# A Trainium2 encoder trunk: head order of the key-query products, and the depth of a low-rank matmul

## Chip, cores and metric

The kernel runs on one core of a Trainium2 chip. The metric is the time of one execution on the device, in microseconds, lower being better. Times of several executions are given by their median. The profile shows one further execution, recorded by the hardware profiler.

## What is computed

Two layers over 2048 tokens of width 1024. Layer A mixes the tokens with a recurrence (RWKV-7), twelve heads of width 64, beside a cross-attention into 256 memory tokens; layer B uses differential attention instead. This case concerns layer A alone:

```python
def rwkv7_time_mix(z, mu, w0, w2, a0, a2, k_k, k_a, r_k, lnx_w, lnx_b):
    ...
    z = z + (token_shift(z) - z) * mu
    r, k, v, wd, ad = jnp.split(z, [BR_W, 2 * BR_W, 3 * BR_W, 3 * BR_W + LORA_W], axis=-1)
    w = -jax.nn.softplus(-(w0 + jnp.tanh(wd) @ w2)) - 0.5
    decay = jnp.exp(-jnp.exp(w))
    a = jax.nn.sigmoid(a0 + ad @ a2)
    ...
    def step(state, inp):
        r_t, w_t, k_t, v_t, kk_t, a_t = inp
        sa = jnp.einsum('bhvk,bhk->bhv', state, -kk_t)
        state = (state * w_t[:, :, None, :]
                 + sa[..., None] * (kk_t * a_t)[:, :, None, :]
                 + v_t[..., None] * k_t[:, :, None, :])
        y_t = jnp.einsum('bhvk,bhk->bhv', state, r_t)
        return state, y_t
```

`tanh(wd) @ w2` and `ad @ a2` are the two low-rank products of depth 64. The kernel computes the recurrence in chunks of 64 tokens: inside a chunk it needs the products of keys with queries, 128x128 for each head.

## The kernel before

Layer A is made of 24 steps. A step takes one pair of heads (two heads are the 128 partitions) and one block of 512 tokens, which is eight chunks. The steps run over two halves of the sequence, in each over six head pairs, and for each pair over two blocks, called b=0 and b=1 here. Weights are loaded for a pair in its b=0 step.

A step has these parts. `p1` (from L312) makes its inputs: projections through `pj` (L174, 24 matmuls of 128x512 each, in three passes of rounded parts: high by high, low by high, high by low), the two low-rank products `lr` (L323, L324), and from them the decays, summed by a scan (L330). `p2` (from L371) makes the key-query products `pg` (L380): for each half g of the eight chunks and each head hh one PSUM bank of four products, which DVE then reads (L383), scaled and masked, into `Gm`; two banks come in turn. It also transposes keys and values. `p3` inverts the small triangular matrices of the chunks: on DVE from L431 to L461, with products on PE of 64x64 (`inv`, L455) and 32x32 (`invz`, L468, which needs the transposed block `Ta` of L461, and `invr`, L474). `p4` (from L482) is the recurrence, eight chunks in a row: `xy` (L493, L496), copied by ACT (L498), `us` (L502), copied by DVE (L503), `sps` (L507), added to the state by DVE (L510), and `xy` of the next chunk. `p5` normalises and writes out.

The code calls, for each i, `p4` and `p5` of step i, `p2` and `p3` of step i+1, and `filler(i+2)`, which does `p1` of step i+2 and a gate projection. A scheduler of the language then sets the order on each engine; each engine works through its own list in order. So on PE the chunks of `p4` have products of other parts between them, which cover the waits for ACT and DVE. PSUM has eight banks: two for `pg` and the other small results, two for `xy`, one for `us` and `sps`, three for `pj` and `lr`.

The low-rank operands: `th[i]` (128x512) holds the high part of one input and its low part, in 64 rows each (`lora_in`). `load_lora` (L568) makes a tile `lora` of three 128x128 slots: slots 0 and 1 are the high parts of `w2` and `a2`, each twice, one above the other; slot 2 holds the low part of `w2` in rows 0 to 63 and that of `a2` in rows 64 to 127. So L323 multiplies the weights' high part by the input's high and low, over 128 rows, and L324 adds the weights' low part by the input's high, over 64 rows.

Of the kernel before, what the change touches and what calls it, by code (L numbers as in the profile page):

```python
# [15 lines left out]
P = 128  # L16
# [9 lines left out]
TB = 512  # L26
# [33 lines left out]
def hybrid_kernel(ctx, tc, S, HALF, x, mem, pv, cv, dist, postn, w_out, w_mkv, a_w, w2, a2, w_kv, b_w, out):  # L60
# [47 lines left out]
    def split_w(pool, src, gain, hi, lo, eng=G_, raws=None, tag="wraw", bufs=RAWS):  # L108
        """weights from DRAM as hi + lo"""
# [19 lines left out]
    def rstd_(xt, junk, ss):  # L129
        """junk: where the squares go; ss: a column for each part of the rows"""  # L130
        for i, (x_, j_) in enumerate(zip(xt, junk)):
            A.activation(j_, x_, AF.Square, accum_out=ss[:, i:i + 1])
        if len(xt) > 1:
            V.tensor_tensor(out=ss[:, 0:1], in0=ss[:, 0:1], in1=ss[:, 1:2], op=ALU.add)

    def rows_T(xt, ps, dst, eng):
        """512 columns of 128 rows, transposed, to each hi, lo of dst, with its gain; eng rounds to hi"""
# [13 lines left out]
    def norm_T(rows, dst, pool, W, PS, xt=None, ptag="gm", eng=nc.sync, junk=None):  # L151
        """128 rows of DRAM (or xt), normalised and transposed into each hi, lo of dst, with its gain"""
# [26 lines left out]
    def mem_T(h, m0, W, PS, pool):  # L179
        """the memory, normalised for both layers, transposed"""  # L180
# [4 lines left out]
    def mem_kv(h, tile_, W, load, PS):  # L185
        """for both layers, keys (hi over lo) and values of the memory, to DRAM"""
# [22 lines left out]
    def layer_a(ph):  # L209
# [96 lines left out]
        class Step:  # L306
            """one head pair, one block of TB tokens"""
# [4 lines left out]
            def p1(self):  # L312
# [7 lines left out]
                for i, e in enumerate((cum[:, :, 1:65], asg.rearrange("p (c t) -> p c t", t=C))):  # L320
                    pl = PS([P, TB], "lr", "pj")
                    rows = slice(i * 64, i * 64 + 64)
                    mm(pl, lhsT=lora[:, i], rhs=th[i], start=True, stop=False)  # L323
                    mm(pl, lhsT=lora[rows, 2], rhs=th[i][rows], start=False, stop=True)  # L324
# [24 lines left out]
                # AR: even chunk (r|a), odd (a|r);  BK: even (k|b), odd (b|k)  # L349
# [7 lines left out]
                # 1 + (a - 1) k_a  # L357
# [13 lines left out]
            def p2(self):  # L371
                p, rn, AR, BK = self.p, self.rn, self.AR, self.BK
                Gm = T([P, 2, NJ, 2, P], "Gm", 2)
                for g in range(2):
                    for hh in range(2):
                        pg = PS([P, 4, P], "pg")
                        hs = slice(hh * 64, hh * 64 + 64)
                        for c4 in range(4):
                            c = g * 4 + c4
                            mm(pg[:, c4, :], lhsT=BK[hs, c, :], rhs=AR[hs, c, :], start=True, stop=True)  # L380
                        for c4 in range(4):
                            c = g * 4 + c4
                            V.scalar_tensor_tensor(out=Gm[:, c % 2, c // 2, hh, :], in0=pg[:, c4, :], scalar=rn[:, c, hh:hh + 1],  # L383
                                                   in1=cc("maskE" if c % 2 == 0 else "maskO", 128), op0=ALU.mult, op1=ALU.mult)
                # BK transposed, rows scaled
# [23 lines left out]
            def p3(self):  # L409
                Gm = self.Gm  # L410
                # N = strict upper part: odd rows 0:64 cols 0:64, even rows 64:128 cols 64:128
# [22 lines left out]
                # X1[p, t, (ib, i)] = T[t, i];  X2[p, i, (tb, t)] = T[t, i]  # L434
# [11 lines left out]
                # TT32 = TT16 + TT16 E1 TT16, E1 between the 16 x 16 blocks of each 32 x 32 one  # L446
# [12 lines left out]
                # the 32 x 32 blocks a (first) and b of each chunk: TT[a, b] = TT[a, a] N[a, b] TT[b, b]  # L459
# [22 lines left out]
            def p4(self):  # L482
# [3 lines left out]
                for c in range(NC):  # L486
                    j, e = c // 2, c % 2
                    ar = slice(64, 128) if e == 0 else slice(0, 64)   # alpha / U rows
                    rr = slice(0, 64) if e == 0 else slice(64, 128)   # r / V rows
# [62 lines left out]
        def lora_in(w18, half, b):  # L552
# [7 lines left out]
            # hi over lo for the one, lo over hi for the other  # L560
# [7 lines left out]
        def load_lora(p):  # L568
            """hi of both, twice; lo of the one over lo of the other"""
# [4 lines left out]
            l = pw.tile([P, 3, P], F32R, name="lora", tag="lora", bufs=1)  # L574
            A.activation(l[:, 0:2], raw, AF.Copy)
            for i in range(2):
                rows = slice(i * 64, i * 64 + 64)
                G_.tensor_tensor(out=l[rows, 2], in0=raw[rows, i], in1=l[rows, i].bitcast(F32), op=ALU.subtract)
# [5 lines left out]
        def filler(idx):  # L584
            """what the lookahead of step idx traces: its inputs and projections"""
# [96 lines left out]
    def store_q(l, m, b, ps, gate, W):  # L682
        """queries (hi, lo) and gates of two heads of the memory attention, TB tokens, to DRAM"""
# [593 lines left out]
```

## Time and profile before

| | |
|---|---|
| three runs | 3231.21, 3232.57 and 3237.78 us; median 3232.57 us |
| profiled execution, span | 3242.7 us, its own time; 10.1 us above the median |
| PE busy | 3074.5 us, 95% of the span |
| DVE, ACT, POOL busy | 2008.1, 1421.3, 928.4 us |
| chain that ended last | PE 76%, DVE 14%, ACT 4% |
| mean granted TensorE clock | 0.977 of full |

PE (TensorE) is the engine of the matmuls, DVE VectorE, ACT ScalarE, POOL GpSimd. The busy times overlap; the chain that ended last is followed back from the last instruction, at each step to what released it. L380 means line 380 of the kernel. Layer A takes about the first 1560 us of the span.

### The profile page before, as it was taken

The page shows a single profiled execution, that of the slowest core. Times are in us where ns is not written, and L with a number is a line of the kernel's source. Part 1 is how long each engine was busy: PE and PEld are TensorE (multiplying, and loading weights), DVE is VectorE, ACT ScalarE, POOL GpSimd, SP SyncE. Part 2 cuts the span into 40 slices and gives each one's busy share as a digit, 9 for nine tenths or more (in the row PEclk, how much of TensorE's full clock was granted, in tenths as well). Part 3 has the DMA queues.
Part 4 walks back from the last instruction along what each step waited for, and adds up shares of the span by engine and source line. Part 5 has one row for each costly group of instructions (what it writes and reads, how often), then busy time and mean ns, then how long its engine had stood idle before and what let it go on. Part 6 is the DMA issues. An engine that isn't in the chain of part 4 may idle for free.

```text
span 3242.7 us, 53751 instructions
## 1 busy us (share of the span) xinstructions
PE 3074.5 (95%) x20026; PEld 2404.1 (74%) x20026; DVE 2008.1 (62%) x5546; ACT 1421.3 (44%) x3126; POOL 928.4 (29%) x1092
## 2 busy tenths in 40 slices
PE   6899999998899999999899999999999999999999
PEld 4766767676667676767577798898887878877777
DVE  6678777866687878786456411111106888887554
ACT  6524333434443434333345522222315777777443
POOL 3224434443244334433100121312411332222100
PEclk9989999998899999999899999999999999999999
DMA  4201000113210001002554443423436555444453
GB/s 131 75 16 35 27 22 22 34 40 90 57 35 27 23 22 33 29 18 69 136 147 135 134 113 90 117 74 96 117 110 159 118 116 112 102 85 119 118 154 113
DMA packets 266150, 265.21 MB, mean 82 GB/s; under 512 B 16832, under 2 KB 206656, under 8 KB 265760
## 3 DMA queue, kind: packets, MB, share of 16 engines
q1 hardware_dynamic: 237760, 195.31, 20.7%
q0 software_dynamic: 28128, 66.46, 10.1%
q8 instruction: 157, 2.57, 0.3%
q14 instruction: 105, 0.86, 0.1%
HBM read 180.45 MB, written 81.26 MB: 81 GB/s over the span
## 4 chain that ended last, share of the span: by engine, by line
PE 76%; DVE 14%; ACT 4%; issue 3%; DMA 2%; POOL 1%; SPq 0%; DVEq 0%; ACTq 0%; POOLq 0%
PE pj L174 30%; PE po L820 10%; PE o L1135 5%; PE vps L996 4%; PE pg L380 3%; PE s L1094 3%; PE s L1095 2%; PE us L502 2%; PE xy L496 2%; PE tr L1125 2%; PE sps L507 1%; PE xy L493 1%; PE mo L759 1%; PE xy L513 1%; DVE E L1097 1%
## 5 line engine op out<-in xcount | busy, mean ns | idle before, releaser
L174 PE MATMUL pj<-hhi,wh 128*128 128x512 f32 x928 | 395.3, 426 | 2.2 <-DVE hlo L149 1.7
L174 PE MATMUL pj<-hhi,wl 128*128 128x512 f32 x928 | 393.2, 424 | 0.4 <-POOL wl L123 0.4
L174 PE MATMUL pj<-hlo,wh 128*128 128x512 f32 x928 | 385.0, 415 | 0.0
L123 POOL TENSOR_TENSOR wl<-wraw,wh 128x512 fp32r<-128x512 f32 x168 | 221.0, 1327 | 399.8 <-ACT wh L122 372.2
L1097 DVE CUSTOM_DVE_ANT_0 E<-s,dist 128x512 f32<-128x512 f32 (+1 forms) x480 | 276.2, 605 | 35.0 <-PE s L1095 28.9
L174 PE MATMUL pj<-bh,wh 128*128 128x512 f32 x672 | 262.6, 391 | 0.0
L174 PE MATMUL pj<-bl,wh 128*128 128x512 f32 x672 | 262.4, 391 | 0.0
L174 PE MATMUL pj<-bh,wl 128*128 128x512 f32 x672 | 262.3, 390 | 0.0
L1102 ACT ACTIVATE E<-E,nm 128x1920 f32<-128x1920 f32 (+7 forms) x192 | 229.4, 1199 | 59.1 <-DVE nm L1100 58.6
L491 POOL TENSOR_SCALAR SP<-sb,PC 128x128 f32<-128x128 f32 x192 | 119.5, 624 | 469.7 <-DVE sb L510 469.7
L1135 PE MATMUL o<-th,vs 128*128 128x256 f32 (+1 forms) x864 | 211.0, 376 | 2.3 <-ACT th L1128 0.9
L174 PEld LDWEIGHTS pj<-hhi,wh 128*128 128x128 f32 x928 | 178.5, 192 | 45.6 <-ACT hhi L148 3.3
L1094 PE MATMUL s<-ks,qd 128*128 128x512 f32 (+1 forms) x480 | 205.7, 432 | 2.2 <-DVE mx L1097 1.2
L174 PEld LDWEIGHTS pj<-hhi,wl 128*128 128x128 f32 x928 | 177.6, 191 | 38.9 <-POOL wl L123 0.8
L174 PEld LDWEIGHTS pj<-hlo,wh 128*128 128x128 f32 x928 | 178.2, 192 | 33.9 <-issue 0.2
L122 ACT ACTIVATE wh<-wraw 128x512 fp32r<-128x512 f32 x168 | 105.4, 628 | 198.0 <-PE pj L174 138.9
L1135 PEld LDWEIGHTS o<-th,vs 128*128 128x128 f32 x864 | 153.8, 189 | 38.7 <-ACT th L1128 19.4
L514 ACT ACTIVATE ys<-xy 64x128 f32<-64x128 f32 x192 | 52.0, 271 | 297.0 <-PE xy L513 251.5
L1095 PE MATMUL s<-ks,qd 128*128 128x512 f32 (+1 forms) x480 | 176.2, 373 | 0.0
L510 DVE SCALAR_TENSOR_TENSOR sb<-sps,PC,SP 64x64 f32<-64x64 f32 x384 | 108.4, 282 | 64.9 <-PE sps L507 57.0
L174 PEld LDWEIGHTS pj<-bh,wh 128*128 128x128 f32 x672 | 126.6, 188 | 26.4 <-DVE ot L831 0.3
L174 PEld LDWEIGHTS pj<-bl,wh 128*128 128x128 f32 x672 | 126.6, 188 | 26.2
(401 smaller groups left out, 7342.3 us busy)
## 6 DMA issues: line engine op xcount, KB each, us to landing
wraw<-in_a_w SPq DMA_DIRECT2D x126, 256.0 KB, 2.9
qd<-qd_d POOLq DMA_DIRECT2D x48, 512.0 KB, 6.9
mq<-mq POOLq DMA_DIRECT2D x64, 256.0 KB, 4.3
ks<-ks_d POOLq DMA_DIRECT2D x24, 512.0 KB, 6.5
yr<-y_dram SPq DMA_DIRECT2D x31, 384.0 KB, 4.9
xt<-in_x SPq DMA_DIRECT2D x16, 512.0 KB, 5.3
x_dram<-ot SPq DMA_DIRECT2D x16, 512.0 KB, 4.4
wraw<-in_b_w SPq DMA_DIRECT2D x32, 256.0 KB, 3.0
```

Of the source, the lines that this page charges most:

```text
L122: A.activation(hi[:, ks], raw, AF.Copy)
L123: eng.tensor_tensor(out=lo[:, ks], in0=raw, in1=hi[:, ks].bitcast(F32), op=ALU.subtract)
L174: mm(ps, lhsT=w[a_][:, k, wcol], rhs=h[b_][:, k, tsl], start=n == 0, stop=n == 3 * KT - 1)
L491: G_.tensor_scalar(out=SP, in0=SB, scalar1=PC[:, c:c + 1], scalar2=None, op0=ALU.mult)
L510: V.scalar_tensor_tensor(out=SB[hc, hc], in0=sp[hc, :], scalar=PC[hc, c:c + 1], in1=SP[hc, hc], op0=ALU.mult, op1=ALU.add)
L820: mm(po[hf], lhsT=a_[:, k, :], rhs=b_[hf][:, k, :], start=k == i == 0, stop=k == KT - 1 and i == 2)
L996: mm(ps[:, t, :], lhsT=hT[b][a_][:, k, tsl], rhs=w[b_][:, k, :], start=n == 0, stop=n == 3 * KT - 1)
L1094: mm(ps[:, f:f + w_], lhsT=qd[:, 0, c, qs], rhs=k_[:, c, 0:w_], start=True, stop=False)
L1095: mm(ps[:, f:f + w_], lhsT=qd[:, 1, c, qs], rhs=k_[:, c, 0:w_], start=False, stop=True)
L1097: V.tensor_tensor_reduce(out=e[:, kb * 512:kb * 512 + w], in0=ps[:, 0:w], in1=dt_[:, u0:u0 + w], scale=-SLOPES[h], scalar=3.0e38, op0=ALU. ...
L1102: A.activation(E[c][:, 0:nk], E[c][:, 0:nk], AF.Exp, bias=nm[:, c:c + 1], scale=-1.0, accum_out=nm[:, 2 + c:3 + c])
L1135: mm(po[:, oc], lhsT=vs[kt // 4][:, kt % 4, :], rhs=th[:, rc], start=n == 0, stop=n >= nmm - 2, skip_group_check=True)
```

## The change

There are three parts. In `p2` both banks of a half are allocated together and the matmuls take the two heads in turn; DVE's readings keep their order, head 0's four and then head 1's four. In `p1` and `load_lora` the second low-rank matmul uses 128 rows: the tile has four slots, slots 2 and 3 hold the low parts of `w2` and `a2`, each twice, and the product gains the term low by low. One POOL subtraction over 128x256 takes the place of two over 64x128. And `ones` and `epsd`, two small constants of layer B, come from a pool that is opened behind layer A; the two DVE operations that fill them then run there. The line numbers of the changed kernel are smaller by one in `p1` from L323 on (L323, L324 and L330 are now L322, L323 and L329); L380 is now L379, and L383 to L513 differ by at most one. Comments that went are left out here.

```diff
                 for i, e in enumerate((cum[:, :, 1:65], asg.rearrange("p (c t) -> p c t", t=C))):
                     pl = PS([P, TB], "lr", "pj")
-                    rows = slice(i * 64, i * 64 + 64)
                     mm(pl, lhsT=lora[:, i], rhs=th[i], start=True, stop=False)
-                    mm(pl, lhsT=lora[rows, 2], rhs=th[i][rows], start=False, stop=True)
+                    mm(pl, lhsT=lora[:, 2 + i], rhs=th[i], start=False, stop=True)
...
                 for g in range(2):
+                    pgs = [PS([P, 4, P], "pg") for hh in range(2)]
+                    for c4 in range(4):
+                        for hh in range(2):
+                            hs = slice(hh * 64, hh * 64 + 64)
+                            mm(pgs[hh][:, c4, :], lhsT=BK[hs, g * 4 + c4, :], rhs=AR[hs, g * 4 + c4, :], start=True, stop=True)
                     for hh in range(2):
-                        pg = PS([P, 4, P], "pg")
-                        hs = slice(hh * 64, hh * 64 + 64)
                         for c4 in range(4):
                             c = g * 4 + c4
-                            mm(pg[:, c4, :], lhsT=BK[hs, c, :], rhs=AR[hs, c, :], start=True, stop=True)
-                        for c4 in range(4):
-                            c = g * 4 + c4
-                            V.scalar_tensor_tensor(out=Gm[:, c % 2, c // 2, hh, :], in0=pg[:, c4, :], scalar=rn[:, c, hh:hh + 1],
+                            V.scalar_tensor_tensor(out=Gm[:, c % 2, c // 2, hh, :], in0=pgs[hh][:, c4, :], scalar=rn[:, c, hh:hh + 1],
                                                    in1=cc("maskE" if c % 2 == 0 else "maskO", 128), op0=ALU.mult, op1=ALU.mult)
...
-            l = pw.tile([P, 3, P], F32R, name="lora", tag="lora", bufs=1)
+            l = pw.tile([P, 4, P], F32R, name="lora", tag="lora", bufs=1)
             A.activation(l[:, 0:2], raw, AF.Copy)
-            for i in range(2):
-                rows = slice(i * 64, i * 64 + 64)
-                G_.tensor_tensor(out=l[rows, 2], in0=raw[rows, i], in1=l[rows, i].bitcast(F32), op=ALU.subtract)
+            G_.tensor_tensor(out=l[:, 2:4], in0=raw, in1=l[:, 0:2].bitcast(F32), op=ALU.subtract)
...
-    ones = const.tile([P, P], F32, name="ones")
-    epsd = const.tile([P, P], F32, name="epsd")
...
     op = layer_a(ph.enter_context(pool_(name="ph", bufs=NB)))
+    const2 = ctx.enter_context(pool_(name="const2", bufs=1, side="right"))
+    ones = const2.tile([P, P], F32, name="ones")
+    epsd = const2.tile([P, P], F32, name="epsd")
```

What the scheduler makes of it is seen in the order of instructions on an engine. First PE, at the start of a stretch of the recurrence beside which a b=0 step is prepared. The names are those of the code, with numbers of the buffers: two numbers of `pg` are the two heads' banks. Before:

```order
L380 MATMUL pg_5911<-AR_5648,BK_5649 128x128 x3
L502 MATMUL us_5729<-xs_5727,TT_5419 64x64 x2
L380 MATMUL pg_5911<-AR_5648,BK_5649 128x128
L380 MATMUL pg_5920<-AR_5648,BK_5649 128x128 x4
L507 MATMUL sps_5733<-UV_5338,BKT_5325 64x64 x2
...
L380 MATMUL pg_5929<-AR_5648,BK_5649 128x128
L502 MATMUL us_5749<-xs_5747,TT_5419 64x64 x2
L380 MATMUL pg_5929<-AR_5648,BK_5649 128x128 x3
L507 MATMUL sps_5753<-UV_5338,BKT_5325 64x64 x2
L513 MATMUL xy_5743<-UV_5338,Gm_5288 64x64 x2
L380 MATMUL pg_5938<-AR_5648,BK_5649 128x128 x4
```

And now:

```order
L379 MATMUL pg_5904<-AR_5641,BK_5642 128x128
L379 MATMUL pg_5905<-AR_5641,BK_5642 128x128
L379 MATMUL pg_5904<-AR_5641,BK_5642 128x128
L502 MATMUL us_5722<-xs_5720,TT_5413 64x64 x2
L379 MATMUL pg_5905<-AR_5641,BK_5642 128x128
L379 MATMUL pg_5904<-AR_5641,BK_5642 128x128
L379 MATMUL pg_5905<-AR_5641,BK_5642 128x128
L379 MATMUL pg_5904<-AR_5641,BK_5642 128x128
L379 MATMUL pg_5905<-AR_5641,BK_5642 128x128
...
L379 MATMUL pg_5922<-AR_5641,BK_5642 128x128 x3
...
L379 MATMUL pg_5923<-AR_5641,BK_5642 128x128 x3
...
L379 MATMUL pg_5923<-AR_5641,BK_5642 128x128
```

In the first half (5911 and 5920 before, 5904 and 5905 now) the heads alternate; in the second half (5929 and 5938 before, 5922 and 5923 now) head 0's four still come ahead of head 1's four, and head 1's four are now parted by the next chunk.

Second, PE at the end of such a stretch, behind the last `sps` of a step. Before:

```order
L507 MATMUL sps<-UV,BKT 64x64 x2
...
L323 MATMUL lr<-th_1322,lora 128x512
L324 MATMUL lr<-th_1322,lora 128x512
L323 MATMUL lr<-th_1325,lora 128x512
L324 MATMUL lr<-th_1325,lora 128x512
L174 MATMUL pj<-hhi,wh 128x512
...
L455 MATMUL inv<-T_3645,E_3585 64x64 x9
L535 MATMUL py<-cvt,ys 128x128 x4
L455 MATMUL inv<-T_3645,E_3585 64x64 x7
...
L455 MATMUL inv<-TT_3649,E_3585 64x64 x16
...
L468 MATMUL invz<-Ta,Gm 32x32 x16
```

And now:

```order
L507 MATMUL sps<-UV,BKT 64x64 x2
...
L322 MATMUL lr<-th_1319,lora 128x512
L323 MATMUL lr<-th_1319,lora 128x512
L322 MATMUL lr<-th_1322,lora 128x512
L323 MATMUL lr<-th_1322,lora 128x512
L174 MATMUL pj<-hhi,wh 128x512
...
L535 MATMUL py<-cvt,ys 128x128 x4
...
L455 MATMUL inv<-T_3640,E_3580 64x64 x16
...
L455 MATMUL inv<-TT_3644,E_3580 64x64 x16
...
L468 MATMUL invz<-Ta,Gm 32x32 x16
```

Ahead of the first `inv`, six products `pj` stood behind `lr`, and eleven stand there now, ten of them ahead of `py`, which is no longer in the middle of `inv`; between the second `inv` and `invz` there were six and are eight.

Third, DVE in the same kind of stretch, where the inverse's last step and the decays' scan (L330, now L329) meet. Before:

```order
L326 TENSOR_SCALAR cum<-cum 128x8x64
L282 COPY carry<-pj 128x1
L326 TENSOR_SCALAR asg<-asg 128x512
L458 TENSOR_TENSOR TT<-inv,TT_6039 128x512
L461 STREAM_TRANSPOSE Ta<-TT 128x256
L330 SCALAR_TENSOR_TENSOR cum<-cvt,cum 128x520
L335 TENSOR_SCALAR kk<-kx,pvt 128x512
```

And now:

```order
L325 TENSOR_SCALAR cum<-cum 128x8x64
L325 TENSOR_SCALAR asg<-asg 128x512
L458 TENSOR_TENSOR TT<-inv,TT_6032 128x512
L329 SCALAR_TENSOR_TENSOR cum<-cvt,cum 128x520
L461 STREAM_TRANSPOSE Ta<-TT 128x256
L334 TENSOR_SCALAR kk<-kx,pvt 128x512
```

The scan stood behind the transpose `Ta` and stands ahead of it.

## Rows read from the trace of the kernel before

**Rows 1.** The page: span, busy times, chain that ended last by engine.

```profile
span 3242.7 us, 53751 instructions
...
PE 3074.5 (95%) x20026; PEld 2404.1 (74%) x20026; DVE 2008.1 (62%) x5546; ACT 1421.3 (44%) x3126; POOL 928.4 (29%) x1092
...
PE 76%; DVE 14%; ACT 4%; issue 3%; DMA 2%; POOL 1%; SPq 0%; DVEq 0%; ACTq 0%; POOLq 0%
```

**Rows 2.** Windows, three stretches: window, us, busy of each engine, clock, DMA, GB/s.

```profile
492.40:550.90 58.50, 55.42 (x439) 40.32 (x438) 44.39 (x130) 20.15 (x44) 23.01 (x26) 0.94 0.08 24
550.90:604.40 53.50, 52.03 (x440) 37.81 (x439) 44.03 (x125) 20.54 (x46) 20.87 (x26) 1.00 0.09 28
604.40:659.80 55.40, 52.36 (x439) 37.94 (x438) 44.22 (x130) 20.11 (x44) 22.34 (x26) 1.00 0.09 28
```

**Rows 3.** The same view, two windows of 6.90 us behind L468.

```profile
430.00:436.90 6.90, 6.90 (x59) 5.45 (x60) 4.64 (x12) 0.64 (x1) 3.30 (x3) 0.51 0.01 2
...
321.00:327.90 6.90, 6.90 (x75) 5.55 (x75) 4.65 (x12) 1.34 (x3) 3.44 (x3) 1.00 0.01 2
```

**Rows 4.** PE timeline ahead of rows 3: start, us, operation, [idle before <-releaser].

```profile
428.42 0.69 PE L468 MATMUL invz<-Ta,Gm 32*32 32x32 f32 x32 [1.27 <-DVE Ta L461]
```

**Rows 5.** Groups by line: busy us, mean ns, idle us before and its releasers.

```profile
L380 PE MATMUL pg<-AR,BK 64*128 64x128 f32 x768 | 117.3, 297 | 3.6 <-DVE AR L365 3.2 <-DVE Gm L383 0.4
...
L383 DVE SCALAR_TENSOR_TENSOR Gm<-pg,rn,cvt 128x128 f32<-128x128 f32 x384 | 111.7, 343 | 17.9 <-PE pg L380 15.6
...
L578 POOL TENSOR_TENSOR lora<-lraw,lora 64x128 fp32r<-64x128 f32 x24 | 11.1, 462 | 25.4 <-ACT lora L575 24.5
```

**Rows 6.** Timeline of PE, start of a b=0 stretch.

```profile
551.59 0.93 PE L380 MATMUL pg<-AR,BK 64*128 64x128 f32 x6
552.45 0.44 PE L502 MATMUL us<-xs,TT 64*64 64x64 f32 x4
552.82 1.16 PE L380 MATMUL pg<-AR,BK 64*128 64x128 f32 x10
553.91 0.34 PE L507 MATMUL sps<-UV,BKT 128*64 128x64 f32 x4
...
558.63 1.16 PE L380 MATMUL pg<-AR,BK 64*128 64x128 f32 x8
559.72 0.50 PE L174 MATMUL pj<-hlo,wh 128*128 128x512 f32 x1
```

**Rows 7.** Timeline of PE, end of a b=0 stretch.

```profile
584.51 0.49 PE L324 MATMUL lr<-th,lora 64*128 64x512 f32 x1
...
585.84 0.50 PE L174 MATMUL pj<-hhi,wh 128*128 128x512 f32 x1
586.18 0.40 PE L174 MATMUL pj<-hlo,wh 128*128 128x512 f32 x1
586.42 0.39 PE L174 MATMUL pj<-hhi,wl 128*128 128x512 f32 x1
...
594.95 0.69 PE L468 MATMUL invz<-Ta,Gm 32*32 32x32 f32 x32 [0.56 <-DVE Ta L461]
```

**Rows 8.** Timeline of PE, end of a b=1 stretch.

```profile
641.24 0.50 PE L324 MATMUL lr<-th,lora 64*128 64x512 f32 x1
...
652.26 0.69 PE L468 MATMUL invz<-Ta,Gm 32*32 32x32 f32 x32 [1.25 <-DVE Ta L461]
```

**Rows 9.** Timeline of DVE, end of these two stretches.

```profile
583.80 0.58 DVE L510 SCALAR_TENSOR_TENSOR sb<-sps,PC,SP 64x64 f32<-64x64 f32 x2 [0.33 <-PE sps L507]
...
592.29 1.43 DVE L326 TENSOR_SCALAR asg<-asg 128x512 f32<-128x512 f32 x1
...
595.00 1.24 DVE L330 TENSOR_TENSOR_SCAN cum<-cvt,cum 128x520 f32<-128x520 f32 x1 [0.20 <-ACT cum L328]
...
641.20 0.58 DVE L510 SCALAR_TENSOR_TENSOR sb<-sps,PC,SP 64x64 f32<-64x64 f32 x2 [0.47 <-PE sps L507]
...
648.15 0.40 DVE L326 TENSOR_SCALAR asg<-asg 128x512 f32<-128x512 f32 x1
```

## The prediction

> **What bounds the kernel.** I read the page first [rows 1]: in a span of 3242.7 us TensorE (PE) is busy for 3074.5 us, and PE holds 76% of the chain that ended last, VectorE (DVE) 14%. So a microsecond less on PE is worth most of a microsecond, except where DVE is what PE waits for. The change touches only layer A's 24 steps, so next I cut that layer into stretches, one for each step of the recurrence, from the first L493 of a step to the first L493 of the next [rows 2]. There are two kinds, in turn. When the recurrence runs beside the preparation of a b=0 step, the stretch lasts 53.5 us at full granted clock; all eight in the middle of the layer do so within 0.1 us. Beside a b=1 step it lasts 55.4 us at full clock or 58.5 us with a mean clock of 0.94: of nine, four are long, and the other five stand within 0.2 us of 55.4. PE is busy for 52.03 of 53.5 us and for 52.36 of 55.4 us, and this is where the change must act.
>
> The long ones come from the clock [rows 3]: of 6.90 us in which PE is busy throughout, one stretch had a granted clock of 0.51 (1.2 GHz) and did 59 matmuls, its undisturbed counterpart had 1.00 (2.4 GHz) and did 75. The price is the difference of the stretches, 58.5 − 55.4 = 3.1 us a fall. PE had just waited 1.27 us for Ta and then done the 32x32 products of L468 [rows 4].
>
> **Part 1, key-query products.** Each product of L380 is two instructions. The table shows 768 of them at a mean of 297 ns [rows 5], but they are pipelined, so I price runs by the distance from one start to the next [rows 6]: six instructions (three products of one head) take 552.45 − 551.59 = 0.86 us; eight (four of one head) 559.72 − 558.63 = 1.09; ten (one product of head 0, then four of head 1) also take 553.91 − 552.82 = 1.09. Thus another product of the same head costs 0.23, and a product of the other head beside it nothing: the two heads' operands lie in different halves of the rows. A run costs 0.40 + 0.23 (n − 1), n being the larger count of one head.
>
> The order lists show where alternation really arises. Of each step's two halves only g=0 alternates; in g=1 the second bank is not free yet, and head 0's four still come first. A b=1 step goes from AAAAB|BBB|AA|AA|BBB|B to ABABA|BAB|AA|AA|BBB|B: the first two runs cost 1.09 + 0.86 before and 0.86 + 0.63 now, 0.46 less. A b=0 step goes from AAA|ABBBB|A|AAA|BBBB to ABA|BABAB|A|AAA|BBB|B: 0.23 + 0.23 less, but the last four are split, which costs 0.86 + 0.40 − 1.09 = 0.17 more. Over all 24 steps these runs sum to 104.8 us before and 95.9 after: −8.9. The ten runs that are added cost another 0.1 each, since the first projection product after a change of shape starts 0.34 us before the next instead of 0.24 [rows 7]: **−7.9 us**. The bounds: if an alternated product of the other head rides free less often than in the row, nothing is gained and ten splits of 0.17 + 0.1 cost 2.7 us; at the other end −8.9. I take the figure near the upper end, since the row shows the very case.
>
> DVE's eight readings of a half's two banks take 8 × 0.343 = 2.7 us [rows 5]. They stay in their order, and PE's idle time ahead of L380 because of them is 0.4 us in the whole run. What the products hide is the recurrence's round trips through ScalarE (ACT) and DVE: the 0.86 us of filling between L496 and L502 [rows 6] becomes 0.63. PE's total idle time for that reason is small, and other chunks live with less.
>
> **Part 2, the low-rank products.** The second matmul has 64 rows before and 128 after. With alternating shapes three of them take (585.84 − 584.51) / 3 = 0.44 us each, against 0.24 for a projection product behind one of its own shape [rows 7]. Four in a step become cheaper by 0.2: 0.8 us a step, 19 us in 24 steps, gross. How much stays depends on where they stand.
>
> In b=1 stretches only the last of the four, the second L324, stands behind the last L507 [rows 8], and DVE waited 0.47 us for that product [rows 9]. Then DVE has work without a gap until Ta, and PE takes up L468 at 652.26, 11.1 us after DVE's 641.20, having waited 1.25 us. So only what comes ahead of L507 is kept, two cheaper instructions, about 0.4, and at most the 0.47 that DVE waited: taken as 0.5 × 10 = **−5 us**. The fourth one's saving only lengthens the wait.
>
> In b=0 stretches all four come behind the last L507, and from 583.80 to 594.95 DVE sets the pace again, 11.15 us [rows 7, 9]; there the saving itself is worth nothing. But the scheduler fills differently: eleven projection products instead of six stand between L324 and L455 and eight instead of six right ahead of L468, and six fewer remain behind it: 6 × 0.23 = −1.4. Against this the scan, 1.24 us, now comes ahead of Ta on DVE; but the L326 ahead of it, which takes 1.43 us here because its input comes late from ACT, gets it earlier and can shrink towards the 0.40 of its twin [rows 9], so I estimate L468 at 1.24 − 1.03 = 0.2 later. One more change of shape costs about 0.3. Sum −0.9, × 10 = **−9 us**. Bounds: L468 later by the whole scan, +0.2 a step (+2); not later at all, −1.1 (−11). I stay near the low end, since the late input is in the row. Four other steps (ends of the halves): −0.4 each, −1.6.
>
> **Part 3, small things.** Two POOL subtractions of 462 ns [rows 5] become one over 128x256: between 0.46 us (as one now) and 1.85 (by size), at most +0.9 in each of 12 loads, on an engine that is busy for 29% [rows 1]; a step's weights come two steps ahead, and that lead covers it. Gone the lead, 12 × 0.9 = 11 us. `ones` and `epsd` move to the start of layer B: two DVE operations once, under 1 us. Zero for all.
>
> **Part 4, what it triggers.** By the working above the b=0 stretches meet L468 with PE idle for some 1.2 us, where they idled 0.56 us before and never lost the clock; the b=1 ones show what idling 1.25 us does: four falls in nine. I take three more falls, 3 × 3.1 = **+9 us**, bounds none and eleven.
>
> The Trainium skill (TensorE: Matmul & The Clock Gate) says that idle gaps let the clock fall; the trace agrees that it fell behind a gap of 1.27 us [rows 4], and shows that 1.25 us can also pass without one [rows 8].
>
> **Sum:** −7.9 − 5 − 9 − 1.6 + 9 = −14.5, which I round to −13.5 for the products I could not place. The profiled span lies 10 us above the median of the runs, 3232.6; the terms hold there as well, so 3232.6 − 13.5 = **3219 us**. About 0.2%, 6.5 us, is what a measurement of this kernel tells from no change.
>
> **Rivals.**
> (a) *The savings hold and no clock is lost*: −7.9 − 5 − 9 − 1.6 = −23.5, less some loss, 3209; with a fall or two fewer, 3205. For it: falls hang on a small shift in time, and never happened in b=0 stretches. Against: a longer wait. 0.17.
> (b) *DVE's stretch absorbs part 2*: the scan delays Ta in full, +2 in place of −9, and one fall fewer: −7.9 − 5 + 2 − 1.6 + 6 = −6.5, 3226. For it: DVE has no gap there. 0.14.
> (c) *The readings of the two banks become the bound*: if DVE's 2.7 us for a half hold back the next half's products, part 1's −7.9 is lost: 3227. Against: the 0.4 us of waiting above. 0.09. The Trainium skill (TensorEngine Tiling (Array Packing), PSUM Bottleneck) states this rule: packing speeds up TensorE and not the emptying of PSUM, which may become the bottleneck.
> (d) *The change does not do what it says*: heads that alternate don't overlap, +2.7 in place of −7.9: 3229. Against: the ten-instruction run. 0.06.
> (e) *Slower*: the longer wait ahead of L468 drops the clock in nearly every stretch. With eleven new falls (34 us) against −23.5: +10.6, 3243; it decides from eight new falls on. For it: 1.25 us already does so in four of nine, and b=1 waits grow by 0.3. Against: five of nine at the same wait did not fall. 0.14.
> The forecast: 0.40.
>
> **Numbers.** Faster by over 0.2% (below 3226.1): the forecast's 0.40, (a) 0.17, and a little of (b): 0.59. Within: the rest of (b), (c), (d): 0.27. Slower: (e): 0.14. The range from 3200 to 3238 leaves out (e) and a little below (a).
>
> **What would show it.** Right: stretches beside b=1 steps near 54.4 us where the clock is full, beside b=0 steps near 52.3 with PE idle over 1 us ahead of L468; runs of L379 with five products in 0.86 us; L322 and L323 0.24 apart. Wrong: alternated runs that cost 0.23 for every product; idle time ahead of L379 released by Gm, or ahead of L502 by xs; Ta later than 11.2 us behind the last sb; a granted clock near 0.94 in most stretches.

## The result and the profile after

The changed kernel took 3265.9 us (median of three runs, 3263.63 to 3274.35) against 3232.57 us: the ratio is 1.0107, with a 95% interval of 1.0083 to 1.0130. It is slower by 33 us, where 13.5 us less had been forecast. The profiled executions stand at 3242.7 us before and 3261.9 us after, so this pair shows 19 of the 33 us. The page of the kernel after begins:

```profile
span 3261.9 us, 53730 instructions
...
PE 3073.8 (94%) x20026; PEld 2410.4 (74%) x20026; DVE 1990.7 (61%) x5546; ACT 1417.2 (43%) x3126; POOL 919.0 (28%) x1080
```

TensorE does the same 20026 matmuls and is busy for as long as before [rows 1]; what grew is the span. The sum hides two things that the windows further down show apart: in a b=0 stretch PE is busy for 51.64 us where the clock holds, less than the 52.03 of before [rows 2], and for 54.69 where it falls. The two parts that were to make matmuls cheaper did so. The timeline of PE shows, first, the start of a b=0 stretch, then the low-rank products, then L468:

```profile
552.20 0.71 PE L379 MATMUL pg<-AR,BK 64*128 64x128 f32 x6
552.83 0.44 PE L502 MATMUL us<-xs,TT 64*64 64x64 f32 x4
553.21 0.93 PE L379 MATMUL pg<-AR,BK 64*128 64x128 f32 x10
554.07 0.33 PE L507 MATMUL sps<-UV,BKT 128*64 128x64 f32 x4
...
584.99 0.39 PE L323 MATMUL lr<-th,lora 128*128 128x512 f32 x1
585.22 0.40 PE L322 MATMUL lr<-th,lora 128*128 128x512 f32 x1
...
597.68 0.69 PE L468 MATMUL invz<-Ta,Gm 32*32 32x32 f32 x32 [1.98 <-DVE Ta L461]
```

Six instructions of alternating heads take 0.63 us from start to start, ten take 0.86, against 0.86 and 1.09 [rows 6]; low-rank products start 0.23 us apart, against 0.44 [rows 7]. But PE, which waited 0.56 us ahead of L468 in such a stretch [rows 7], now waits 1.98. DVE's readings of the two banks do not hold PE up, 1.1 us in the whole run, in the group by line:

```profile
L379 PE MATMUL pg<-AR,BK 64*128 64x128 f32 x768 | 108.0, 300 | 5.8 <-DVE AR L364 4.7 <-DVE Gm L383 1.1
```

The timelines of DVE, POOL and ACT in the same stretch as above say why L468 is late:

```profile
584.61 0.58 DVE L510 SCALAR_TENSOR_TENSOR sb<-sps,PC,SP 64x64 f32<-64x64 f32 x2 [0.42 <-PE sps L507]
...
593.16 1.50 DVE L325 TENSOR_SCALAR asg<-asg 128x512 f32<-128x512 f32 x1
594.59 0.68 DVE L458 TENSOR_TENSOR TT<-inv,TT 128x512 f32<-128x512 f32 x1
595.95 1.24 DVE L329 TENSOR_TENSOR_SCAN cum<-cvt,cum 128x520 f32<-128x520 f32 x1 [0.69 <-ACT cum L327]
597.11 0.42 DVE L461 STREAM_TRANSPOSE Ta<-TT 128x256 f32<-128x256 f32 x1
```

```profile
592.93 1.46 POOL L539 TENSOR_TENSOR ys<-ys,sil 128x512 f32<-128x512 f32 x1 [1.17 <-DVE ys L538]
```

```profile
594.70 0.63 ACT L326 ACTIVATE asg<-asg 128x512 f32<-128x512 f32 x1 [0.80 <-DVE asg L325]
595.24 0.61 ACT L327 ACTIVATE cum<-cum 128x512 f32<-128x512 f32 x1
```

The scan stands ahead of Ta, DVE waits another 0.69 us for its input, and L468 starts 597.68 − 584.61 = 13.07 us after the last sb instead of 11.15 [rows 7, 9]: 1.92 us later, and 1.24 for the scan and 0.69 for its wait make 1.93. L325 takes 1.50 us, as it did before (1.43), beside a product on POOL that begins just ahead of it. It holds back the scan too: ACT does L326 on asg, for which it had waited 0.80 us until L325 was done, ahead of L327, which finishes the scan's input cum.

The windows show the stretches of the kernel after, a b=1 one without a loss of clock, a b=0 one and a b=1 one with it, and a b=0 one without (columns as in rows 2):

```profile
264.30:318.70 54.40, 51.32 (x440) 37.50 (x439) 44.53 (x128) 20.12 (x44) 22.35 (x26) 1.00 0.08 24
...
436.50:494.20 57.70, 54.69 (x439) 39.66 (x438) 42.26 (x127) 20.25 (x46) 22.67 (x27) 0.94 0.10 29
494.20:551.50 57.30, 54.30 (x439) 39.83 (x438) 43.46 (x127) 20.14 (x44) 21.48 (x26) 0.94 0.07 22
551.50:606.10 54.60, 51.64 (x440) 37.56 (x439) 41.87 (x124) 20.30 (x46) 20.25 (x25) 1.00 0.10 30
```

Of the seventeen stretches in the middle of the two halves, four lost the clock before, all beside b=1 steps. Now ten falls begin there, in seven of nine stretches beside b=1 steps and three of eight beside b=0 steps. Nine of the ten begin within 2.1 us of the start of an L468 that had waited 1.26 to 2.02 us. One of them, in the timeline of PE and in windows around it, clock falling from 1.00 to 0.50 for 10.2 us:

```profile
365.03 0.83 PE L468 MATMUL invz<-Ta,Gm 32*32 32x32 f32 x32 [2.02 <-DVE Ta L461]
```

```profile
363.00:365.40 2.40, 0.38 (x24) 0.40 (x25) 2.09 (x5) 1.54 (x4) 0.00 (x0) 1.00 0.29 109
365.40:375.60 10.20, 10.20 (x85) 7.32 (x78) 4.32 (x12) 3.45 (x7) 5.01 (x4) 0.50 0.18 53
```

The account of the profiled pair, from the windows of all stretches: the seventeen together last 938.6 us before and 963.7 after, +25.1. The mean b=0 stretch without a fall went from 53.52 (of eight) to 54.66 (of five); for eight stretches that is +9.1. The mean b=1 stretch without a fall went from 55.33 (of five) to 54.55 (of two); for nine, −7.0. What is above those levels, the cost of the falls, went from 12.4 to 35.4: +23.0. The rest of layer A, mostly the start and the passage between the halves, gave back 5.9 (one such piece alone lasts from 115 to 127 us in the kernels below, in no order that the changes explain), and what follows layer A is the same within 0.3 us. The other 14 us of the difference of medians are not in this pair: before, the three timed runs took 5 to 12 us less than the span of the profiled execution. Where falls land changes from execution to execution; that the timed runs of before had fewer of them fits, but isn't shown for these three.

### The profile page after: what moved, and what is told of

The parts are those of the page before. It is cut to its first block, busy times and chain, and to the rows that moved or that the text cites. A ratio compares the mean times of both kernels' runs of the same rounds, so it can differ in the third digit from the quotient of the medians.

```text
span 3261.9 us, 53730 instructions
## 1 busy us (share of the span) xinstructions
PE 3073.8 (94%) x20026; PEld 2410.4 (74%) x20026; DVE 1990.7 (61%) x5546; ACT 1417.2 (43%) x3126; POOL 919.0 (28%) x1080
## 5 line engine op out<-in xcount | busy, mean ns | idle before, releaser
L174 PE MATMUL pj<-hlo,wh 128*128 128x512 f32 x928 | 394.9, 425 | 0.0
L174 PEld LDWEIGHTS pj<-bh,wl 128*128 128x128 f32 x672 | 126.3, 188 | 26.2
```

The lines of the kernel that those rows point to most:

```text
L174: mm(ps, lhsT=w[a_][:, k, wcol], rhs=h[b_][:, k, tsl], start=n == 0, stop=n == 3 * KT - 1)
```

## The experiments

Among e1 to e5, the scheduler gives TensorE the order of the kernel before, apart from the products themselves, wherever these do not alternate strictly in b=0 steps, and the order after wherever they do. So the order could be parted from the edits. In the table, b=0 and b=1 are mean lengths without a fall, the wait is the one ahead of L468, and low clock is the time at about half clock within the seventeen stretches of the profiled execution.

| kernel | median us | ratio to before (95%) | b=0, wait | b=1, wait | low clock |
|---|---|---|---|---|---|
| before | 3232.57 | | 53.5, 0.5 | 55.3, 1.3 | 27 us |
| after | 3265.9 | 1.0107 (1.0083 to 1.0130) | 54.7, 2.0 | 54.6, 1.3 | 79 us |
| e1, heads only | 3268.16 | 1.0112 (1.0087 to 1.0137) | 54.8, 2.0 | 55.1, 1.3 | 65 us |
| e2, low-rank only | 3241.29 | 1.0017 (1.0001 to 1.0034) | 53.3, 0.3 | 55.0, 1.3 | 31 us |
| e3, heads in b=1 steps | 3231.34 | 0.9986 (0.9969 to 1.0002) | 53.3, 0.3 | 54.6, 1.3 | 41 us |
| e4, heads in b=0 steps | 3270.39 | 1.0107 (1.0084 to 1.0129) | 54.6, 2.0 | 54.9, 1.3 | 61 us |
| e5, two products swapped | 3224.99 | 0.9964 (0.9949 to 0.9979) | 52.9, 0.3 | 54.6, 1.3 | 34 us |
| e6, wait filled | 3239.71 | 1.0007 (0.9992 to 1.0023) | 52.9, 0.3 | 55.7, none | 3 us |
| e8, e5 and gate on DVE | 3235.2 | 0.9995 (0.9975 to 1.0014) | 52.5, none | 53.8 (two), 0.6 | 55 us |
| e9, after and gate on DVE | 3216.96 | 0.9959 (0.9939 to 0.9978) | 53.5, 0.7 | 54.0, 0.6 | 14 us |
| e10, before and gate on DVE | 3266.13 | 1.0088 (1.0053 to 1.0123) | 52.9, none | 59.7 (fallen), 0.5 | 102 us |

Each ratio is to runs of the kernel before on the same chip, whose medians there were 3234.3 to 3236.3 us; that of the kernel after is to the three runs above. In e9 and e10 the first b=1 stretch of the second half takes in work that otherwise lies in the passage between the halves (75.7 and 68.9 us); it is left out of their b=1 figures.

The waits and the falls can be counted over these profiled executions. Of 21 b=0 stretches with a wait of 2.0 us ahead of L468 (after, e1, e4), in 13 the clock fell within 3 us of L468's start; of 63 b=1 stretches with a wait of 1.3 us (before, after, e1 to e5), in 23; of 73 stretches of either kind with a wait of 0.3 to 0.75 us, in none.

**e1, the heads alone.** The p2 hunk of the diff, and nothing else.

> The head order of the key-query products alone; the low-rank products and the constants are as in the kernel before. The order of all other instructions on TensorE is that of the changed kernel. Theory A (the loss is the new order: in b=0 stretches the scan now stands ahead of Ta on DVE, L468 comes later, and the longer wait lets the clock fall more often): slower by most of the 33 us, 3250 to 3270 us; in the profile b=0 stretches of 54.5 to 55.5 us without a fall, a wait of about 2 us ahead of L468, some 8 to 10 falls in the even middle of layer A against 4. Theory B (the loss comes from the low-rank products, whose saving only lengthens the wait for Ta): near 3232 - 8 = 3225 us, 4 falls. Theory C (both leave PE waiting longer, each gives falls): about 3245 us.

3268.16 us: the heads alone make the whole loss, with the same wait of 2.0 us and eight falls, five of them beside b=0 steps. Theory A.

**e2, the low-rank products alone.** The other hunks, without the p2 one.

> The low-rank products over 128 rows alone, with the constants moved (the four-slot tile needs their room); key-query products as before. The order on TensorE is that of the kernel before, instruction by instruction. Theory A: about 5 us less from the b=1 stretches (0.5 us each, 54.9 us without a fall), nothing in the b=0 ones (53.5 us): 3226 to 3230 us. Theory B: slower, 3245 to 3265 us, with 8 or more falls. Theory C: about 3245 us.

3241.29 us, within 0.2% of before in the ratio and above what theory A expected. The profile shows the gain by stretch: 55.33 to 55.00 beside b=1 steps, 53.52 to 53.32 beside b=0 steps. The windows of one of each:

```profile
487.74:542.82 55.08, 51.83 (x440) 37.88 (x438) 44.28 (x130) 20.13 (x44) 22.37 (x26) 1.00 0.09 25
542.82:596.04 53.22, 51.41 (x439) 37.82 (x438) 43.74 (x125) 20.30 (x46) 21.38 (x26) 1.00 0.10 28
```

These 0.3 and 0.2 us do not show in the timed runs: a fall more or less weighs ten times as much. The twelve timed runs had a median granted clock of 0.975, against 0.978 in 23 runs of before on the same chip, so they had more time at the low clock; where in the span, the one profile doesn't show. Theory B is out by its time and its falls, five against the 8 it asked for; between A and a small loss this run does not decide.

**e3 and e4, alternation in one kind of step.** All of the change, with this edit of the changed kernel (the multiplying line, left out here, is only indented anew):

```diff
-                    for c4 in range(4):
-                        for hh in range(2):
-                            hs = slice(hh * 64, hh * 64 + 64)
+                    alt = self.t0 // TB % 2 == 1
+                    for u in range(8):
+                        c4, hh = (u // 2, u % 2) if alt else (u % 4, u // 4)
+                        hs = slice(hh * 64, hh * 64 + 64)
```

and `== 0` in e4.

> All of the change, but the heads alternate only in b=1 steps. TensorE's order is then that of the kernel before apart from the alternated products, and the scan stands behind Ta in b=0 stretches. Theory A: b=0 stretches of 53.5 us with a wait of 0.6 us ahead of L468 and no falls, b=1 stretches of 54.4 us where the clock holds: 3217 to 3228 us, faster than both kernels. Theory B: as slow as the whole change, 3250 to 3265 us. Theory C: about 3240 us.

> All of the change, but the heads alternate only in b=0 steps. TensorE's order in the b=0 stretches is that of the changed kernel (scan ahead of Ta); in b=1 steps the products stand as before. Theory A: as slow as the whole change or 5 us more, 3255 to 3275 us, b=0 stretches of 54.6 us or, with a fall, 58 us. Theory B: no different from the low-rank products alone. Theory C: about 3250 us.

3231.34 and 3270.39 us. Alternation in b=1 steps costs nothing: b=1 stretches go from 55.00 in e2 to 54.56, 0.44 us less. Alternation in b=0 steps, which brings the other order, costs everything. e3 missed the expected range by 3 us, and its five falls are not fewer than before's four: the b=1 wait of 1.3 us is still there, and two of the five begin behind it.

**e5, the order of two products swapped in b=0 steps.** The last four of a half's eight products come as A B B instead of B A B behind an A; that keeps the heads alternating almost as well, and the scheduler returns to the old order.

```diff
-                    for c4 in range(4):
-                        for hh in range(2):
+                    for c4, hh in ([(0, 0), (0, 1), (1, 0), (1, 1), (2, 0), (2, 1), (3, 0), (3, 1)] if self.t0 // TB % 2 == 1 else [(0, 0), (0, 1), (1, 0), (1, 1), (2, 0), (3, 0), (2, 1), (3, 1)]):
```

> The whole change, with one difference: in b=0 steps the products of a half are asked for in the order ABABAABB instead of ABABABAB (A head 0, B head 1), b=1 steps alternate throughout. With that the scheduler gives b=0 stretches the order of the kernel before again: scan behind Ta, py inside inv, 6 + 5 + 6 projection products ahead of L468. Theory A (the new order makes the loss): b=0 stretches of 52.8 to 53.2 us, a wait of 0.3 us ahead of L468, no falls there; b=1 stretches as with the heads alternating there alone; 3222 to 3231 us. Theory D (heads that alternate in b=0 steps cost time by themselves, through the PSUM banks or DVE's readings, whatever the order of the rest): 3255 to 3270 us, as the whole change.

3224.99 us, ratio 0.9964 (0.9949 to 0.9979), faster than both kernels, inside the range. One b=1 stretch without a fall, and two beside b=0 steps:

```profile
377.14:431.76 54.62, 51.38 (x439) 37.49 (x438) 44.30 (x130) 20.13 (x44) 22.30 (x26) 1.00 0.09 26
431.76:484.55 52.79, 51.01 (x439) 37.35 (x438) 43.72 (x125) 20.31 (x46) 21.38 (x26) 1.00 0.09 28
...
542.22:594.97 52.75, 50.95 (x440) 37.35 (x438) 43.72 (x125) 20.30 (x46) 20.72 (x25) 1.00 0.09 28
```

Nearly the same sharing of rows as in the changed kernel, and 41 us less by the medians: the loss is the order that came with the edit. Theory D falls.

**e6, PE kept busy through the wait.** e5, and behind the allocation of L468's result

```diff
+                for u in range(24 if self.t0 // TB % 2 else 0):
+                    mm(pz.rearrange("p j h t -> p (j h t)")[:, 0:256], lhsT=self.h[0][:, 0, 0:P], rhs=self.h[0][:, 0, 0:256], start=True, stop=True)
```

> The kernel of e5_swap_two, and in b=1 steps 24 more matmuls of 128x256 that write where L468's result will be written, and are overwritten by it; they take PE through the 1.3 us in which it waits for Ta. The scheduler moves seven projection products behind L468 for it, which costs 1.6 us a stretch. If the falls follow the wait: no fall in b=1 stretches, all of them near 56 us (against 54.5 without and 57.6 to 59 with a fall): 3216 to 3228 us. If they do not: as many falls as in e5_swap_two and 10 to 15 us more than it, 3235 to 3245 us.

The timeline of PE shows L469 (L468 before) taken up without a wait:

```profile
526.79 3.13 PE L463 MATMUL invz<-hhi 128*128 128x256 f32 x24
529.87 0.69 PE L469 MATMUL invz<-Ta,Gm 32*32 32x32 f32 x32
```

In the profiled execution not one fall begins behind L468, in nine b=1 stretches where e5 had three; one of 3.4 us is left, elsewhere in a stretch. Without the wait there was no fall behind it. The stretches are 55.7 us, as expected. But the time, 3239.71 us, is 12 us above the range of that outcome and lies in the range of the other one, and 7 us above the time of the profiled execution (3232.77). The clock recorded with each run says what kind of loss the 7 us are: 0.981 in the profiled one, 0.978 in the three runs of 3239.1 to 3239.7 us. So the timed runs had low clock that the profile doesn't have; where in the span isn't shown, and that no fall stands behind L468 is shown by this one profile alone.

**e7, the scan held behind Ta.** e5, and in `p1`

```diff
-                G_.memset(cum[:, :, 0:1], 0.0)
+                if prev is None:
+                    G_.memset(cum[:, :, 0:1], 0.0)
+                else:
+                    G_.tensor_scalar(out=cum[:, :, 0:1], in0=prev.Ta[:, :, :, 0:1].rearrange("p j h t -> p (j h) t"), scalar1=0.0, scalar2=None, op0=ALU.mult)
```

where `prev` is the step before (none for the first steps).

> The kernel of e5_swap_two, with the scan of every step held behind the Ta of the step before (the zeros at the head of its input are made from Ta times zero by POOL). The scheduler then lays out both kinds of stretch anew: lr later, pss later, more projection products behind py. Theory A and falls that follow the wait: L468 waits under 0.5 us in both kinds, few or no falls, 3205 to 3225 us; unless the later scan makes AR and BK late for the first products of the next step: then waits of 1 to 2 us ahead of L378 in every stretch and 3225 to 3250 us.

3513.3 us, ratio 1.0846 (1.0821 to 1.0871): a miss by a wide margin. The wait ahead of L468 is gone, but everything behind the scan is late, and PE waits for it at the start of the next stretch, 2.65 us in the row below (the product of L404 before); then the clock stays at half for some 27 us:

```profile
620.35 2.07 PE L406 MATMUL pbn<-kx,rkb 128*128 128x512 f32 x2 [2.65 <-POOL kx L368]
```

```profile
620.10:647.40 27.30, 27.05 (x115) 18.99 (x116) 11.28 (x38) 1.91 (x7) 3.17 (x6) 0.50 0.00 1
```

So the scan can't simply be moved back: it feeds the products of the next step. As a test of the scan's place alone it says nothing, since the scheduler laid out the whole stretch anew.

**e8, e9 and e10, the gate product on DVE.** One line, in e5, in the changed kernel and in the kernel before:

```diff
-                G_.tensor_tensor(out=yo, in0=yo, in1=sil, op=ALU.mult)
+                V.tensor_tensor(out=yo, in0=yo, in1=sil, op=ALU.mult)
```

> The kernel of e5_swap_two, with the product of y and its gate (L539 of the kernel before, 1.4 us on POOL, ahead of the output's DMA) moved to DVE. Theory E (the long L326 of 1.43 us in b=0 stretches and the long scan of 2.29 us in b=1 stretches are long because POOL works on L539 at the same time, not because their input is late): L326 near 0.40 us and the scan near 1.24 us in both kinds, DVE gains about 0.7 for the product itself, Ta comes about 0.4 us earlier, the wait ahead of L468 in b=1 stretches falls from 1.3 to about 0.7 us (one projection product more stands ahead of it), fewer falls; 3215 to 3226 us. Theory F (the inputs are late): L326 and the scan keep their lengths, Ta comes 0.7 us later, waits of about 2 us, more falls, 3230 to 3250 us.

> The whole change with the same move of the gate product to DVE; the order around Ta in b=0 stretches stays that of the changed kernel (scan ahead of Ta). Theory E: L325 takes 0.4 instead of 1.5 us, so Ta comes about 0.4 to 1 us earlier in b=0 stretches, their wait ahead of L468 falls from 2.0 to 1.0 to 1.6 us, 54.2 us without a fall; falls somewhat fewer; 3240 to 3258 us: the scan ahead of Ta alone still costs. Theory F: Ta 0.7 us later, waits of 2.7 us in b=0 stretches, 3270 to 3285 us.

> The kernel before with nothing but the gate product moved from POOL to DVE. b=0 stretches have the scan behind Ta, as in e8_sil_dve_order_before. If the gain of e9_sil_dve_order_after over the kernel before is the move's alone, this one is as fast: 3215 to 3220 us. If the change adds its own part once the wait for Ta is short (0.5 us a stretch from the products and 0.5 from the low-rank ones, some 15 us): 3228 to 3240 us, with the new wait of about 1.2 us for BK ahead of L380 at the start of b=1 stretches that e8_sil_dve_order_before showed, and short falls behind it.

On DVE both theories can be read off by line. The scan's mean fell from 1624 ns in the changed kernel to 1269 ns in e9, and `asg`:

```profile
L329 DVE TENSOR_TENSOR_SCAN cum<-cvt,cum 128x520 f32<-128x520 f32 x24 | 30.5, 1269 | 4.4 <-ACT cum L327 4.4
...
L539 DVE TENSOR_TENSOR ys<-ys,sil 128x512 f32<-128x512 f32 x24 | 16.3, 678 | 0.0
...
L325 DVE TENSOR_SCALAR asg<-asg 128x512 f32<-128x512 f32 x24 | 9.9, 412 | 0.2 <-ACT asg L324 0.2
```

Theory E: 412 ns, in place of 847 on average and 1.50 us in the b=0 stretch above; e8 and e10 have 412 too. Beside b=1 steps it was the scan that was long. The timelines of DVE and POOL in the kernel before:

```profile
648.50 2.29 DVE L330 TENSOR_TENSOR_SCAN cum<-cvt,cum 128x520 f32<-128x520 f32 x1
```

```profile
648.31 1.38 POOL L539 TENSOR_TENSOR ys<-ys,sil 128x512 f32<-128x512 f32 x1 [1.52 <-DVE ys L538]
```

The Trainium skill (SBUF — State Buffer, "SBUF: two separate sides") says that DVE and GpSimd share one pair of ports as an exclusive lock: of a GpSimd instruction and a DVE one that needs the pair (in a two-port mode, or with two inputs in SBUF while GpSimd reads SBUF) the first to start keeps it for its whole instruction, and the other is blocked. By that rule such a DVE instruction behind L539 waits till it ends, and the trace agrees: L325 started 0.23 us after L539 and ended 0.27 us after it, the scan started 0.19 us after it and ended 1.10 us after it, each close to its own length of 0.40 and 1.24 us. Whether L325, with one such input, runs in a two-port mode no run here shows.

e9, which keeps the scan ahead of Ta, took 3216.96 us, the lowest median here, ratio 0.9959 (0.9939 to 0.9978, which overlaps e5's interval), and 23 us better than the best that was expected of it. In its b=0 stretches TensorE's order is that of the changed kernel, instruction by instruction, but the scan no longer waits for ACT, and PE waits 0.73 us ahead of L468:

```profile
577.90 1.23 DVE L329 TENSOR_TENSOR_SCAN cum<-cvt,cum 128x520 f32<-128x520 f32 x1
579.04 0.42 DVE L461 STREAM_TRANSPOSE Ta<-TT 128x256 f32<-128x256 f32 x1
```

```profile
579.61 0.69 PE L468 MATMUL invz<-Ta,Gm 32*32 32x32 f32 x32 [0.73 <-DVE Ta L461]
```

No b=0 stretch lost the clock, and none of the four falls in the seventeen stretches begins behind L468. So the new order of TensorE by itself is not what costs: with the same order and Ta in time the b=0 stretches are 53.5 us, as before the change. The same line in the kernel before (e10) makes it slower by 0.88%, 26 us above the range, and in e5 (e8) gains nothing; e8's time lies in the range of theory F, though DVE's lines are those of theory E. In those two, PE gets to the next step's products before BK is ready, and waits there 1.2 us, as e8's expectation had not foreseen and e10's had only for short falls. The timelines of PE of e8 and of e10, and windows behind them:

```profile
482.09 0.90 PE L378 MATMUL pg<-AR,BK 64*128 64x128 f32 x10 [1.19 <-DVE BK L359]
```

```profile
502.89 1.13 PE L380 MATMUL pg<-AR,BK 64*128 64x128 f32 x10 [1.21 <-DVE BK L360]
```

```profile
484.20:487.60 3.40, 3.40 (x12) 1.25 (x11) 2.11 (x8) 0.27 (x1) 2.74 (x4) 0.51 0.38 101
```

```profile
510.70:520.90 10.20, 10.20 (x46) 7.62 (x46) 4.26 (x15) 0.82 (x3) 1.20 (x2) 0.50 0.00 1
```

A wait of over a microsecond in another place, in eight b=1 stretches of each kernel; seven of e8's lost the clock and all eight of e10's. In e8 the fall mostly begins 1.4 to 2.2 us after the delayed products start, in e10 mostly 7.8 us after (510.7 against 502.89), so that it follows from this wait is argued, not shown. In e9 PE waits 0.69 us at that place in most b=1 stretches, for AR. So the gain of e9 isn't the moved line's alone: it needs the changed kernel's order, in which BK is ready sooner relative to PE.

## Why the prediction was wrong

Point by point:

- **Part 1, key-query products: right.** Runs cost what the formula said: 0.63 for six and 0.86 for ten alternated instructions. Per stretch, alternation gained 0.44 us beside b=1 steps (e3 against e2; 0.46 was forecast) and 0.44 beside b=0 steps with the old order (e5 against e3). DVE's readings of the banks did not become the bound: PE's idle time ahead of L379 put down to Gm is 1.1 us in the whole run, from 0.4 [rows 5]. That is rival (c) settled, and with it the rule of the Trainium skill that the prediction named beside it, "PSUM Bottleneck": no run here shows it to bind.
- **Part 2, low-rank products beside b=1 steps: right in kind**, 0.33 us a stretch (e2 against before) where 0.5 was taken. Beside b=0 steps the saving by itself, held worth nothing, is 0.2. That e2's timed runs had a lower clock (0.975 against 0.978) was not in the sum; its cause stays open.
- **Part 2, the new order of the b=0 stretches: this is the step that failed.** It put L468 later by 1.24 − 1.03 = 0.2 us and the stretch at −0.9. The 1.03 was L326 shrinking "towards the 0.40 of its twin" because its late input would come earlier. The row was misread: L326 was long because POOL's gate product ran beside it, and stayed long (1.50 us; 0.41 once that product had left POOL, in e9). The scan also waited 0.69 us for ACT, which was not in the sum; rows 9 held the sign, since even behind Ta the scan waited 0.20 us for ACT. L468 came 1.92 us later, not 0.2, and the stretch went +1.1. The bound given for this, +0.2 a stretch, took in the scan but nothing queued ahead of it.
- **Part 4, the clock: the kind was right, the size too small.** Three more falls were forecast, all beside b=0 steps, for a wait of 1.2 us there. The wait was 2.0, and the profiled execution has three falls there. That this is the forecast number is luck: e1 and e4, with the same wait, have five each. The other three of the six new falls are beside b=1 steps, where the wait ahead of L468 is 1.3 us before and after and no new fall was forecast. Six of nine such stretches lost the clock behind L468 after the change, four of nine before, 23 of 63 over seven kernels; whether the change has a part in that is not shown. The six cost 23.0 us together. The ten falls cost 3.5 us each on average instead of 3.1, since three of them last 10.2 us and not 6.8.
- **Rival (e)** had the direction: PE waits longer ahead of L468 and the clock falls. It had 0.14, and asked for falls in nearly every stretch. Six more were enough in the profiled execution, because its break-even of eight was worked out with the −23.5 us of savings, in which the b=0 stretches stand with −9 us for ten and measured +9.1 for eight. Rival (b), the scan delaying Ta, put that at no more than +0.2 a stretch.
- **Part 3** fits a cost of nothing: e2 carries both edits and is within 0.2%. It was not tried alone.
- **Two loose readings, without weight in the sum:** seven of the eight b=0 stretches lie within 0.1 us of 53.5, the last one lasts 53.9; and the five full-clock b=1 stretches last 55.16 to 55.47 us.

What stays open, beside what is said to be open above, is the 14 us of the difference of medians that the profiled pair does not show. The granted clocks of later runs bear on it. Of 23 runs of the kernel before on one chip, the three with a mean clock of 0.977 took 3238.3 to 3239.6 us, the three with 0.979 took 3232.0 to 3234.0, and the four with 0.981 took 3226.3 to 3230.8; the profiled execution had 0.977. So a profiled execution with more low clock than the timed runs fits, but the clocks of those three runs are not on record.

## What to carry to other kernels

An edit that makes some matmuls cheaper can change where a scheduler puts everything else; compare the order on the engine that is waited for (here DVE ahead of Ta) before adding up the savings, and try a neighbour of the edit that leaves the order alone (swapping two products was worth 41 us). A long instruction with no wait shown ahead of it should be checked against the engine next to it before it is called late. And a wait on TensorE can cost more than itself once the clock goes with it: behind waits of 1.3 us ahead of L468 23 of 63 stretches lost it, behind 2.0 us 13 of 21, for 6.8 or 10.2 us at half clock each time; behind waits of 0.3 to 0.75 us none of 73 did.

## What the runs showed of the hardware

- DVE beside POOL: a 128x512 TENSOR_SCALAR of 0.40 us took 1.43 to 1.50 us, and a scan of 1.24 us took 2.29, where POOL's 128x512 TENSOR_TENSOR of 1.4 us had started just ahead; with that product on DVE their means are 412 and 1269 ns.
- The two heads' products, on different row halves of TensorE, overlap when they alternate: five alternating products took the 0.86 us that three products of one head took before.
- After nearly the same wait for BK (1.19 and 1.21 us) the clock came back after 3.4 us in most of e8's falls, where heads alternate, and after 10.2 us in most of e10's, where they do not. The falls also begin at different places behind the wait (mostly 1.4 to 2.2 us and 7.8 us), and whether alternation is the reason was not tried by itself.
